# Neighbourhood-attention heads get their own block of 128 rows in DRAM: one load a tile, stores in halves of 64 rows

## The chip, the cores and the metric

The kernel runs on one core of one Trainium2 chip. The metric is device time in microseconds (us) of that core. Before the change the median of 3 runs is 2555.72 us (2554.66 to 2556.14).

## The reference: what is computed

One layer of a trunk over 1024 latent tokens (a 16 x 64 grid) and 256 context tokens, width 1024, all in float32: half a SwiGLU step, then two token mixers on one normalised input, then another half SwiGLU step. The mixers are a two-dimensional neighbourhood attention (8 heads of 64; every latent query looks at a window of 8 x 16 of its grid neighbours, with a bias, and at all 256 context keys, in one softmax) and a latent attention (MLA, 8 heads), joined by sigmoid gates. The part that matters here:

```python
qa, ka, va, cq, ckv, kr, gates = jnp.split(h @ w_in, IN_SPLITS, axis=-1)
...
s_loc = jnp.einsum('bjqhd,bjakhd->bhjqak', q_r, k_b) + bias      # 8 rows x 32 columns of keys, masked to 16
s_ctx = jnp.einsum('bjqhd,bkhd->bhjqk', q_r, k_ctx)
p = jax.nn.softmax(jnp.concatenate([s_loc, s_ctx], axis=-1), axis=-1)
o = einsum('bhjqak,bjakhd->bjqhd', p_loc, v_b) + einsum('bhjqk,bkhd->bjqhd', p[..., n_loc:], v_ctx)
```

Matrix products are made in a reduced format (fp32r) of which a float32 number takes two parts, a high and a low one; a product is made of the parts that matter.

## The kernel before

The program is one straight stream. Two orders matter. Most of it is recorded by a planner (steps of TensorE work, with side work of the other engines and loads spread over them) and pinned: engines execute it in the order in which it was written. The neighbourhood attention's vector and scalar work (lines 1934 to 2027) is written through `nc.vector`, `nc.scalar` and so isn't pinned; a scheduler places it. All loads and stores are issued by SyncE (SP), whose queue is pinned; at most 8 of its transfers are outstanding, since a transfer waits for the one issued 8 before it. A store isn't issued at once: it waits in a list for 2 or 3 steps (or until a load asks for the same tensor), so that SP doesn't stand still for a result.

- **Projections (about 700 to 1180 us of the span).** Units of one weight block each make a 128 x 512 result in a PSUM bank. `emit_q` (line 1376) scales it by 1/8, casts it to the high part `hi` on ScalarE (ACT) and takes the low part `lo` on VectorE (DVE); both are stored in `qas[i]` (pair of heads `i`, 4 pairs, two chunks `ci` of 512 tokens). `emit_k` (line 1394) does the same for keys, in `kas[i]`; `side_k` (line 1605) for the 256 context tokens. In DRAM a tensor of before is [high/low, 128 rows, tokens], and the 128 rows are the 2 x 64 rows of two heads.
- **Neighbourhood attention (about 1284 to 1475 us).** `NaHead.loads` (line 1719) fills a head's tiles. `q` holds the 64 rows of the high queries twice (rows 0 to 63 and 64 to 127), `ql` the low ones twice, `k` the high keys above the low keys, `kvc` the same for context keys and, in its other half, values. So a product over 128 rows adds high x high and high x low at once. A head of 64 rows lies in half of a block of before: every tile takes two loads of 64 rows, 8 a head; the two halves of `k` (256 KB each) come last. Tiles `w` have 6 buffers, two heads of 3.
- **One item** is a quarter of a head (16 columns of the grid), 32 in all. `scores` (line 1971) has TensorE (PE) make for each half s the context scores (`cs`, both halves in one PSUM bank) and the local scores (`loc`, a bank for each half). DVE adds the bias and takes the maximum (line 1995, "I" here, 384 wide), copies the context scores with their maximum (line 1966, "T", 256 wide), joins the maxima (line 2002); ACT makes the exponentials (line 2004). `values` turns the weights by TensorE, splits them (ACT line 2026, DVE line 2027, three times an item: local, context, edge) and weighs the values. `head_out` copies on ACT (lines 1934 to 1938), adds on DVE (line 1939), and multiplies and splits on GpSimd. PE works on scores of a later item while the others finish the earlier. The first three items of head 0 are begun earlier, in the MLA query projection, and use a pool `f`; the scores' bank of one item comes free by the I or T that reads it.
- Loads of the head after next are issued by SP along the items; what SP has to wait for is the release of the tile that they fill.

Of the kernel before, what the change touches and what calls it, by code (L numbers as in the profile page):

```python
# [15 lines left out]
P = 128  # L16
# [3 lines left out]
NLAT = 1024  # L20
# [18 lines left out]
def f32(ap):  # L39
    return ap.bitcast(F32)  # L40
# [3 lines left out]
def hybrid_block(ctx: ExitStack, tc: tile.TileContext, a: dict, out: bass.AP):  # L44
# [11 lines left out]
    def nm(s):  # L56
        count[0] += 1
        return f"{s}_{count[0]}"
# [8 lines left out]
    def U(dt=F32, key="u"):  # L67
        return pools[key].tile([P, 1024], dt, tag="u", name=nm("x" + key))
# [4 lines left out]
    def W(dt=F32R, key="w", n=1024):  # L73
        return pools[key].tile([P, n], dt, tag=key, name=nm(key))

    def T2(dt=F32, n=512):
        return pools["t"].tile([P, n], dt, tag="t", name=nm("t"))
# [4 lines left out]
    def DR(shape):  # L82
        n = nm("d")
        return dp.tile(shape, F32, tag=n, name=n)
# [37 lines left out]
    def ld(dst, src):  # L122
        for x in [x for x in waiting if x[1].tensor.name == src.tensor.name]:
            waiting.remove(x)
            put(*x[1:])
        return put(dst, src)
# [4 lines left out]
    def put(dst, src):  # L131
        return pin(nc.sync.dma_start(dst, src))

    def store(dst, src, n=2):

        if clock[0] is None:
            return put(dst, src)
        waiting.append((clock[0] + n, dst, src))
# [7 lines left out]
    def later(f, n=0):  # L146

        deferred.append((clock[0] + n, f)) if clock[0] is not None else f()
# [1097 lines left out]
    o = len(plan.main)  # L1246
# [7 lines left out]
    e = len(plan.main)  # L1254
# [56 lines left out]
    o = len(plan.main)  # L1311
# [12 lines left out]
    o, tail = down1.plan(plan)  # L1324
# [35 lines left out]


    zs = [DR([P, NLAT]) for _ in range(16)]
    qas = [DR([2, P, NLAT]) for _ in range(4)]
    kas = [DR([2, P, NLAT + NCTX]) for _ in range(4)]

    def emit_gate(i, ci, x, bank):
        t = T2() if bank else x

        def gate():
            act.activation(t, x, AF.Sigmoid, bias=bg[:, i:i + 1])  # L1370
            store(zs[i][:, ci * 512:(ci + 1) * 512], t)
        behind(bank, gate)

    def emit_q(i, ci, x, bank):
        c0 = ci * 512
        t, hi, lo = T2() if bank else x, T2(F32R), T2(F32R)
        tv = t.rearrange("p (r j c) -> p j r c", r=8, j=4)
        hv = hi.rearrange("p (j r c) -> p j r c", j=4, r=8)
        lv = lo.rearrange("p (j r c) -> p j r c", j=4, r=8)

        def high():
            act.activation(t, x, AF.Copy, scale=0.125)
            act.copy(hv, tv)
            store(qas[i][0, :, c0:c0 + 512], f32(hi))
            later(low, 1)

        def low():
            vec.tensor_tensor(lv, tv, f32(hv), op=ALU.subtract)
            store(qas[i][1, :, c0:c0 + 512], f32(lo))
        later(high)  # L1390

    def emit_k(i, c0, n, x, bank=True):
        hi, lo = T2(F32R)[:, :n], T2(F32R)[:, :n]

        def high():
            act.copy(hi, x)
            store(kas[i][0, :, c0:c0 + n], f32(hi))

        def low():
            vec.tensor_tensor(lo, x, f32(hi), op=ALU.subtract)  # L1400
            store(kas[i][1, :, c0:c0 + n], f32(lo))
        if bank:
            high()
            low()
        else:
            later(high)
            later(low, 1)
# [28 lines left out]
    def emit_lat(d, ci, x, bank):  # L1436
        t, sq = T2() if bank else x, T2()

        def high():
            if bank:  # L1440
                act.copy(t, x)
            store(cqT[d][:, ci * 512:(ci + 1) * 512], t)
            act.activation(sq, t, AF.Square)
            later(add, 1)

        def add():
            if ci in squares:
                vec.tensor_tensor(squares[ci], squares[ci], sq, op=ALU.add)
            else:
                squares[ci] = sq  # L1450
        later(high)

    for p in range(3):
        punits.append(Unit(h2, [wc_cols(2 * p), wc_cols(2 * p + 1)],
                           lambda i, ci, x, bank, p=p: emit_lat(2 * p + i, ci, x, bank)))
# [21 lines left out]
    o = len(plan.main)  # L1477
# [23 lines left out]
    e = len(plan.main)  # L1501
# [43 lines left out]
    class Set:  # L1545
# [16 lines left out]
        def loads(self):  # L1562

            return [lambda j=j: self.load(j) for j in range(2)]
# [50 lines left out]
    o = len(plan.main)  # L1615
# [97 lines left out]
    def value_tile(i):  # L1713
        return W(key=("l", "p", "p", "z", "z")[i % 5])

    class NaHead:


        def loads(self, h):
            self.h = h  # L1720
            i, b = h // 2, (h % 2) * 64
            self.q, self.ql, self.k = q, ql, k = [W() for _ in range(3)]
            self.kvc = kvc = W(key="x" if h % 3 == 2 else "kc")
            for s in range(2):
                o = 64 * s
                ld(f32(q[o:o + 64, :]), qas[i][0, b:b + 64, :])
                ld(f32(ql[o:o + 64, :]), qas[i][1, b:b + 64, :])
                ld(f32(kvc[o:o + 64, 0:256]), kas[i][s, b:b + 64, NLAT:])
            for s in range(2):
                ld(f32(k[64 * s:64 * s + 64, :]), kas[i][s, b:b + 64, :NLAT])  # L1730
            self.bias = []
            self.table(0)
            yield
            self.table(1)
            self.va = va = value_tile(2 * h)
            for j in range(2):
                self.values(va, j)
            yield
            self.table(2)
            ld(f32(kvc[:, 256:512]), vcs[h])  # L1740
            yield
            self.vb = vb = value_tile(2 * h + 1)
            for j in range(2, 4):
                self.values(vb, j)
            yield
# [109 lines left out]
    o = va_at  # L1855
# [9 lines left out]
    o = len(plan.main)  # L1865
# [4 lines left out]
    o = len(plan.main)  # L1870
# [3 lines left out]
    o = len(plan.main)  # L1874
# [3 lines left out]
    o = len(plan.main)  # L1878
# [303 lines left out]
    for e in range(2):  # L2182
        e = U(F32R)
# [125 lines left out]
    for d in range(KD):  # L2309
        o = len(plan.main)  # L2310
# [52 lines left out]
    o = len(plan.main)  # L2363
# [13 lines left out]
    o = len(plan.main)  # L2377
# [4 lines left out]
    e = len(plan.main)  # L2382
# [9 lines left out]
    o, tail = down2.plan(plan)  # L2392
# [134 lines left out]
```

## Time and profile before

| what | us |
|---|---|
| median of 3 runs | 2555.72 |
| span of the profiled execution | 2553.0 |
| TensorE busy in it | 2524.7 (99%) |
| VectorE, ScalarE, GpSimd busy | 1904.4, 1238.4, 239.4 |

The profiled execution's span is 2553.0 us; the median of the runs lies 2.7 us above, for what is outside the span. TensorE ran at its full granted clock in all 40 slices of the page. In names of instructions `t`, `xu`, `w`, `bs` are pools (bs, bm, bv: PSUM banks), `d` is any tensor in DRAM, `in_wc` a weight input; a line is often that of a helper (L161 the matmul, L164 the transpose, L120 a recorded vector or scalar operation, L132 the DMA issue).

### The profile page before, as it was taken

To read this page: it belongs to the slowest core of one execution; us is meant where nothing else is said; L and a number is where in the kernel's file an instruction comes from. 1 tells how busy PE (TensorE), PEld (TensorE's weight loads), DVE (VectorE), ACT (ScalarE), POOL (GpSimd) and SP (SyncE) were. 2 spreads that over 40 slices of the span, in tenths; PEclk is the share of its full clock that TensorE was granted. 3 is DMA by queue.
4 is the path that set the end of the run, shared out by engine and by line. 5 is a ranking of instruction groups with operands and counts; after the bars stand their busy time and mean duration, and the time that the engine had idled before them with its cause. 6 is when DMAs were issued, how large, how long until landed. Compare 5 with 4: busy or idle time off the path is not lost.

```text
span 2553.0 us, 38188 instructions
## 1 busy us (share of the span) xinstructions
PE 2524.7 (99%) x13007; PEld 2146.5 (84%) x13007; DVE 1904.4 (75%) x3652; ACT 1238.4 (49%) x2384; POOL 239.4 (9%) x421
## 2 busy tenths in 40 slices
PE   8999999999999999999999999999999999999998
PEld 6888888888888888889889999988888888888887
DVE  5788887898567687874568988886445888777557
ACT  6622223555346643433438888772355322233633
POOL 1000000000002200001006622220030000000000
PEclk9999999999999999999999999999999999999999
DMA  8477765779576665666899823205135667557655
GB/s 314 161 244 234 243 224 188 274 247 294 182 241 221 245 224 188 226 229 203 277 284 249 233 67 77 77 28 214 67 131 179 212 223 236 183 185 259 240 202 194
DMA packets 275477, 523.33 MB, mean 205 GB/s; under 512 B 33425, under 2 KB 84433, under 8 KB 275281
## 3 DMA queue, kind: packets, MB, share of 16 engines
q1 hardware_dynamic: 275280, 520.88, 61.3%
q8 instruction: 103, 1.69, 0.3%
q14 instruction: 94, 0.76, 0.1%
HBM read 375.47 MB, written 145.29 MB: 204 GB/s over the span
## 4 chain that ended last, share of the span: by engine, by line
PE 87%; ACT 5%; DVE 4%; issue 2%; DMA 1%; SPq 0%; POOL 0%; DVEq 0%; POOLq 0%; ACTq 0%
PE bs L161 33%; PE bm L161 30%; PE bv L161 20%; PE bm L164 2%; ACT xu L2105 2%; PE bs L164 1%; DVE xu L1966 1%; DVE t L2132 1%; ACT t L2131 1%; ACT xu L2004 1%; DVE xv L120 1%; DMA xv<-in_wada 0%; ACT t L2105 0%; ACT t L1938 0%; PE bv L164 0%
## 5 line engine op out<-in xcount | busy, mean ns | idle before, releaser
L120 ACT CAST xu<-t 128x512 fp32r<-128x512 f32 x589 | 345.6, 618 | 669.8 <-DVE t L120 556.1
L161 PE MATMUL bm<-xu,xu 128*128 128x512 f32 (+1 forms) x2442 | 596.5, 389 | 0.5 <-ACT t L120 0.4
L161 PEld LDWEIGHTS bm<-xu,xu 128*128 128x128 f32 x2442 | 450.4, 188 | 91.6 <-ACT t L120 1.7
L120 DVE TENSOR_TENSOR xu<-t,xu 128x512 fp32r<-128x512 f32 x589 | 382.8, 686 | 78.3 <-ACT xu L120 78.0
L161 PE MATMUL bs<-xu,xu 128*128 128x512 f32 (+2 forms) x1581 | 388.4, 385 | 0.0
L161 PE MATMUL bs<-xv,xu 128*128 128x512 f32 x1512 | 363.6, 390 | 0.2 <-DVE t L120 0.2
L161 PEld LDWEIGHTS bs<-xu,xu 128*128 128x128 f32 x1581 | 291.9, 188 | 57.8
L161 PE MATMUL bv<-xv,xu 128*128 128x512 f32 x1342 | 336.1, 390 | 0.0
L161 PEld LDWEIGHTS bs<-xv,xu 128*128 128x128 f32 x1512 | 283.6, 188 | 59.5 <-issue 1.0
L161 PEld LDWEIGHTS bv<-xv,xu 128*128 128x128 f32 x1342 | 251.7, 188 | 51.9
L120 DVE TENSOR_TENSOR xu<-xu,xu 128x512 fp32r<-128x512 f32 x282 | 189.5, 687 | 59.9 <-ACT xu L120 58.9
L120 DVE TENSOR_TENSOR t<-t,t 128x512 f32<-128x512 f32 (+4 forms) x350 | 221.0, 634 | 13.9 <-ACT t L120 8.7
L161 PE MATMUL bv<-xu,xu 128*128 128x512 f32 x722 | 191.5, 390 | 0.0
L120 ACT CAST xu<-xu 128x512 fp32r<-128x512 f32 x282 | 169.2, 619 | 15.2 <-DMA xu<-in_f1w 8.9
L120 POOL TENSOR_SCALAR st<-st 128x1 f32<-128x1 f32 x56 | 23.8, 425 | 1581.9 <-ACT t L120 1234.4
L161 PEld LDWEIGHTS bv<-xu,xu 128*128 128x128 f32 x722 | 135.6, 188 | 28.0
L161 PE MATMUL bm<-t,xu 128*128 128x256 f32 (+1 forms) x920 | 156.9, 333 | 0.0
L161 PEld LDWEIGHTS bm<-t,xu 128*128 128x128 f32 x920 | 137.7, 189 | 18.3
L161 PE MATMUL bs<-w,w 96*128 96x512 f32 (+1 forms) x384 | 145.0, 406 | 3.9 <-DVE st L1995 2.1
L2132 DVE TENSOR_TENSOR t<-bm,t 128x512 fp32r<-128x512 f32 x160 | 109.6, 687 | 28.5 <-ACT t L2131 28.1
L164 PE MATMUL bm<-ident,xu 128*128 128x128 f32 x826 | 126.5, 272 | 0.0
L1966 DVE TENSOR_SCALAR_CACHE_REDUCE xu<-bs 128x512 f32<-128x512 f32 (+1 forms) x186 | 110.2, 599 | 2.3 <-PE bs L161 2.1
(256 smaller groups left out, 3376.3 us busy)
## 6 DMA issues: line engine op xcount, KB each, us to landing
d<-t SPq DMA_DIRECT2D x432, 256.0 KB, 2.9
t<-d SPq DMA_DIRECT2D x348, 256.0 KB, 4.9
xu<-in_f1w SPq DMA_DIRECT2D x104, 512.0 KB, 4.4
xu<-in_f2w SPq DMA_DIRECT2D x58, 512.0 KB, 4.6
t<-in_wada SPq DMA_DIRECT2D x112, 256.0 KB, 4.9
t<-in_f1w SPq DMA_DIRECT2D x77, 256.0 KB, 4.8
t<-in_f2w SPq DMA_DIRECT2D x77, 256.0 KB, 5.2
xu<-in_winT SPq DMA_DIRECT2D x36, 512.0 KB, 5.4
```

What stands on the lines that cost most here:

```text
L120: return lambda *x, **y: pin(f(*x, **y))
L161: return pin(nc.tensor.matmul(o, s, m, start=start, stop=stop, skip_group_check=open_group[0]))
L164: return pin(nc.tensor.transpose(o, x, i))
L1966: nc.vector.tensor_scalar(dst, src, 1.0, FMIN, op0=ALU.mult, op1=ALU.max, accum_out=m)
L2004: soft.append(lambda s=s: nc.scalar.activation(pr[s][:, :640], pr[s][:, :640], AF.Exp, bias=n_[:, s:s + 1], accum_out=l[:, s:s + 1]))
L2105: nc.scalar.activation(x, x, AF.Exp, bias=n_[:, s:s + 1], accum_out=l[:, i:i + 1])
L2131: nc.scalar.copy(t[0], pb)
L2132: nc.vector.tensor_tensor(t[1], pb, f32(t[0]), op=ALU.subtract)
```

## The change

`qas[i]` becomes [head of the pair, high/low, 128 rows, tokens], the 128 rows being the head's 64 rows twice. `kas[i]` becomes [head of the pair, 128 rows, tokens], high rows over low rows. A new helper `store_rows` stores a 128 x n result in halves of 64 rows: a query result in 4 stores of 64 x 512 (each half twice), a key result in 2. `NaHead.loads` then needs one load a tile.

```diff
-    qas = [DR([2, P, NLAT]) for _ in range(4)]
+    qas = [DR([2, 2, P, NLAT]) for _ in range(4)]
     kas = [DR([2, P, NLAT + NCTX]) for _ in range(4)]
+
+    def store_rows(dst, c, x, twice, s=0):
+        for e in range(2):
+            for o in range(2) if twice else (s,):
+                store(dst[e][64 * o:64 * o + 64, c], f32(x[64 * e:64 * e + 64, :]))
...
-            store(qas[i][0, :, c0:c0 + 512], f32(hi))
+            store_rows([qas[i][e, 0] for e in range(2)], slice(c0, c0 + 512), hi, True)
...
-            store(kas[i][0, :, c0:c0 + n], f32(hi))
+            store_rows(kas[i], slice(c0, c0 + n), hi, False, 0)
...
-            i, b = h // 2, (h % 2) * 64
+            i = h // 2
...
-            for s in range(2):
-                o = 64 * s
-                ld(f32(q[o:o + 64, :]), qas[i][0, b:b + 64, :])
-                ld(f32(ql[o:o + 64, :]), qas[i][1, b:b + 64, :])
-                ld(f32(kvc[o:o + 64, 0:256]), kas[i][s, b:b + 64, NLAT:])
-            for s in range(2):
-                ld(f32(k[64 * s:64 * s + 64, :]), kas[i][s, b:b + 64, :NLAT])
+            for s, x in enumerate((q, ql)):
+                ld(f32(x), qas[i][h % 2, s])
+            ld(f32(kvc[:, 0:256]), kas[i][h % 2][:, NLAT:])
+            ld(f32(k), kas[i][h % 2][:, :NLAT])
```

In the whole program 16 query stores become 64, 16 + 8 key stores (latent and context) 32 + 16, and 64 loads of the 8 heads 32. The order of TensorE is the same; SP keeps the order of all else.

SP where the second pair's queries of the last projections are stored, before (`t` are the results, `d_317` and `d_316` blocks of `qas`):

```order
L132 DMA xu_9839<-in_winT 128x1024
L132 DMA d_317<-t_9779 128x512
L132 DMA t_9866<-in_wada 128x512
L132 DMA d_317<-t_9780 128x512
L132 DMA d_317<-t_9806 128x512
L132 DMA t_9892<-in_wada 128x512
L132 DMA d_317<-t_9807 128x512
```

and after, in the same place:

```order
L132 DMA xu_9855<-in_winT 128x1024
L132 DMA d_317<-t_9795 64x512 x4
L132 DMA t_9885<-in_wada 128x512
L132 DMA d_317<-t_9796 64x512 x4
L132 DMA d_317<-t_9822 64x512 x4
L132 DMA t_9917<-in_wada 128x512
L132 DMA d_317<-t_9823 64x512 x4
```

Four issues stand where one stood; what lies between them keeps its place. SP at head 2's loads, before (`z` takes values, `y` the bias tables, `x` is this head's `kvc`; `w` in order q, ql, q, ql, k, k):

```order
L132 DMA z_13122<-d_332 128x512
L132 DMA z_13122<-d_333 128x512
L132 DMA w_13250<-d_317 64x1024
L132 DMA w_13251<-d_317 64x1024
L132 DMA x_13253<-d_321 64x256
L132 DMA w_13250<-d_317 64x1024
L132 DMA w_13251<-d_317 64x1024
L132 DMA x_13253<-d_321 64x256
L132 DMA w_13252<-d_321 64x1024 x2
L132 DMA y_13262<-in_bias 128x768
```

and after:

```order
L132 DMA z_13186<-d_332 128x512
L132 DMA z_13186<-d_333 128x512
L132 DMA w_13314<-d_317 128x1024
L132 DMA w_13315<-d_317 128x1024
L132 DMA x_13317<-d_321 128x256
L132 DMA w_13316<-d_321 128x1024
L132 DMA y_13322<-in_bias 128x768
```

The last key load is the fourth behind the two of `z` in place of the eighth. Since the scheduler places the attention's vector work, its order changes too. DVE at the fourth item (the first after the three early ones), before (`t<-bm` is the split of line 2027):

```order
L2027 TENSOR_TENSOR t_13038<-bm_13039,t_13037 128x512
L1966 TENSOR_SCALAR xu_13048,st_13050<-bs_13047 128x256
L2027 TENSOR_TENSOR t_13064<-bm_13065,t_13063 128x512
L1939 TENSOR_TENSOR t_13086<-t_13086,bv_13032 64x256
L2027 TENSOR_TENSOR xu_12900<-bm_13092,xu_12900 128x2x128
L2027 TENSOR_TENSOR t_13112<-bm_13113,t_13111 128x512
L1995 ISA xu_13048,st_13050<-bs_13053,y_12966 128x384
L1995 ISA st_13050 128x1
L1995 ISA xu_13049,st_13050<-bs_13073,y_12966 128x384
L1995 ISA st_13050 128x1
L1966 TENSOR_SCALAR xu_13049,st_13050<-bs_13047 128x256
```

and after (lines stand 2 further on):

```order
L2029 TENSOR_TENSOR t_13102<-bm_13103,t_13101 128x512
L1997 ISA xu_13112,st_13114<-bs_13117,y_13030 128x384
L1997 ISA st_13114 128x1
L1997 ISA xu_13113,st_13114<-bs_13137,y_13030 128x384
L1997 ISA st_13114 128x1
L2029 TENSOR_TENSOR t_13128<-bm_13129,t_13127 128x512
L1968 TENSOR_SCALAR xu_13112,st_13114<-bs_13111 128x256
L1968 TENSOR_SCALAR xu_13113,st_13114<-bs_13111 128x256
L1941 TENSOR_TENSOR t_13150<-t_13150,bv_13096 64x256
L2004 TENSOR_REDUCE st_13115<-st_13114 128x2
```

The item's two I, which stood behind the next item's first split, now stand behind its own first split. In the later items DVE's order before is `t I T I t T` in three of four and `t I T t I T` in the fourth (then line 1939, line 2002 and the edge's split); after, items of `t I I T t T` and of `t I t I T T` alternate.

DVE in the first item of a later head, one of the fourth kind, before:

```order
L2027 TENSOR_TENSOR t_13270<-bm_13271,t_13269 128x512
L1995 ISA xu_13289,st_13291<-bs_13295,y_13262 128x384
L1995 ISA st_13291 128x1
L1966 TENSOR_SCALAR xu_13289,st_13291<-bs_13288 128x256
L2027 TENSOR_TENSOR t_13306<-bm_13307,t_13305 128x512
L1995 ISA xu_13290,st_13291<-bs_13316,y_13262 128x384
L1995 ISA st_13291 128x1
L1966 TENSOR_SCALAR xu_13290,st_13291<-bs_13288 128x256
```

and after:

```order
L2029 TENSOR_TENSOR t_13330<-bm_13331,t_13329 128x512
L1997 ISA xu_13349,st_13351<-bs_13355,y_13322 128x384
L1997 ISA st_13351 128x1
L1997 ISA xu_13350,st_13351<-bs_13376,y_13322 128x384
L1997 ISA st_13351 128x1
L1968 TENSOR_SCALAR xu_13349,st_13351<-bs_13348 128x256
L2029 TENSOR_TENSOR t_13366<-bm_13367,t_13365 128x512
L1968 TENSOR_SCALAR xu_13350,st_13351<-bs_13348 128x256
```

The second I moves ahead of the first T and of the second split; the last T stays last.

## Rows read from the trace of the kernel before

**Rows 1.** The page's busy times.
```profile
PE 2524.7 (99%) x13007; PEld 2146.5 (84%) x13007; DVE 1904.4 (75%) x3652; ACT 1238.4 (49%) x2384; POOL 239.4 (9%) x421
```

**Rows 2.** Busy time by stretch; last columns granted clock, DMA share, GB/s.
```profile
core 0: us, PE busy (x) PEld busy (x) DVE busy (x) ACT busy (x) POOL busy (x), PEclk, DMA share, GB/s
1338.00:1475.00 137.00, 130.58 (x1010) 126.49 (x1010) 124.81 (x428) 121.13 (x290) 90.12 (x172) 1.00 0.87 230
1361.72:1457.89 96.17, 94.06 (x744) 92.12 (x743) 90.33 (x311) 89.80 (x217) 70.40 (x132) 1.00 0.95 246
```

**Rows 3.** Timeline of PE at the start of neighbourhood attention: start, length, work, idle before.
```profile
1347.98 0.50 PE L161 MATMUL bs<-kc,w 128*128 128x256 f32 x2 [2.56 <-DVE st L1995]
...
1358.12 0.60 PE L161 MATMUL bs<-w,w 128*128 128x384 f32 x2 [1.75 <-DMA w<-d]
```

**Rows 4.** Timeline of PE, one wait of the steady part.
```profile
1378.43 0.62 PE L161 MATMUL bs<-w,w 128*128 128x384 f32 x2 [0.69 <-DVE st L1995]
```

**Rows 5.** Timeline of DVE ahead of PE's first wait.
```profile
1346.27 0.42 DVE L2027 TENSOR_TENSOR xu<-bm,xu 128x256 fp32r<-128x256 f32 x1
1346.76 0.69 DVE L2027 TENSOR_TENSOR t<-bm,t 128x512 fp32r<-128x512 f32 x1
1347.36 0.55 DVE L1995 CUSTOM_DVE_ANT_0 xu<-bs,y 128x384 f32<-128x384 f32 x1
...
1347.84 0.55 DVE L1995 CUSTOM_DVE_ANT_0 xu<-bs,y 128x384 f32<-128x384 f32 x1
...
1348.31 0.42 DVE L1966 TENSOR_SCALAR_CACHE_REDUCE xu<-bs 128x256 f32<-128x256 f32 x1
```

**Rows 6.** Chain that ended last, at PE's second wait.
```profile
1349.74 8.24 DMA w<-d
```

**Rows 7.** Timeline of SP, the issues of head 2's loads.
```profile
1344.57 0.80 SPq L132 DMA_DIRECT2D z<-d  x2
1345.41 1.09 SPq L132 DMA_DIRECT2D w<-d  x2
...
1349.10 1.23 SPq L132 DMA_DIRECT2D w<-d  x2
```

**Rows 8.** Busy time by stretch, where rows of 128 or of 64 are loaded.
```profile
1300.00:1310.00 10.00, 10.00 (x72) 9.41 (x71) 5.47 (x16) 2.46 (x5) 0.00 (x0) 1.00 1.06 399
1395.00:1400.00 5.00, 5.00 (x42) 5.00 (x41) 4.91 (x16) 4.41 (x11) 3.68 (x7) 1.00 1.04 200
```

**Rows 9.** Timeline of SP, two runs of stores.
```profile
1229.79 10.13 SPq L132 DMA_DIRECT2D d<-xu  x16
...
1274.71 7.35 SPq L132 DMA_DIRECT2D d<-t  x10
```

**Rows 10.** Busy time by stretch, in the projections of queries and of keys.
```profile
1042.00:1074.00 32.00, 32.00 (x143) 26.49 (x142) 30.10 (x50) 14.92 (x27) 0.00 (x0) 1.00 0.75 239
1071.00:1099.00 28.00, 28.00 (x129) 23.17 (x129) 22.77 (x39) 10.27 (x18) 0.00 (x0) 1.00 0.67 203
```

**Rows 11.** Timeline of SP, first and last query store and the loads behind.
```profile
1042.75 0.33 SPq L132 DMA_DIRECT2D d<-t  x1
...
1065.10 0.32 SPq L132 DMA_DIRECT2D d<-t  x1
1065.51 2.56 SPq L132 DMA_DIRECT2D xu<-in_wc  x4
...
1068.82 2.51 SPq L132 DMA_DIRECT2D xu<-in_wc  x4
```

**Rows 12.** DVE and PE behind those loads.
```profile
1074.96 0.68 DVE L120 TENSOR_TENSOR t<-bs,t 128x512 f32<-128x512 f32 x1
...
1079.23 0.68 DVE L120 TENSOR_TENSOR t<-xu,xu 128x512 f32<-128x512 f32 x1
...
1077.40 2.88 PE L161 MATMUL bs<-xv,xu 128*128 128x512 f32 x12
```

**Rows 13.** DMA issues of that stretch: KB each, median us to landing.
```profile
xu<-in_wc SPq DMA_DIRECT2D x8, 128.0 KB, 2.8
```

More of the change, by code (lines that the diff above doesn't have):

```diff
@@ L1388, in low @@
             vec.tensor_tensor(lv, tv, f32(hv), op=ALU.subtract)
-            store(qas[i][1, :, c0:c0 + 512], f32(lo))
+            store_rows([qas[i][e, 1] for e in range(2)], slice(c0, c0 + 512), lo, True)
         later(high)
@@ L1396, in high @@
             act.copy(hi, x)
-            store(kas[i][0, :, c0:c0 + n], f32(hi))
+            store_rows(kas[i], slice(c0, c0 + n), hi, False, 0)
         def low():
             vec.tensor_tensor(lo, x, f32(hi), op=ALU.subtract)
-            store(kas[i][1, :, c0:c0 + n], f32(lo))
+            store_rows(kas[i], slice(c0, c0 + n), lo, False, 1)
         if bank:
```

## The prediction, made before the changed kernel ran

> **What bounds the kernel now.** First the page's busy times [rows 1]: TensorE (PE) is busy for 2524.7 of 2553.0 us, so it idles 28.3 us in the whole program. Nothing that the change does alters PE's work; it can win only idle time of PE, and it loses what it makes PE wait. Then busy time by stretch: from 1338 to 1475 us, the neighbourhood attention, PE idles 137.00 - 130.58 = 6.4 us [rows 2], and the reader is to see that this is the one place where the changed loads are used. Then PE's timeline there. Two waits make up most of it: 2.56 us at 1347.98 for line 1995 on DVE and 1.75 us ahead of 1358.12 for a load of `w` [rows 3]. The rest, from 1361.72 to 1457.89 (24 items, 4.0 us each), is 96.17 - 94.06 = 2.1 us [rows 2], in three waits of about 0.7 us for line 1995, of which one is shown [rows 4]. The DMA engines are at 0.95 there, but no wait of PE in that stretch is for a load. Last the projections, where the stores go: from 1042 to 1074 PE is busy all of 32.00 us and DVE 30.10, with the DMA engines at 0.75 [rows 10]. A late load there stops DVE and soon PE; there is no idle time to take it up.
>
> **The wait for a load (1.75 us).** The chain of waits shows the second half of head 2's `k`, 8.24 us on its way from 1349.74 [rows 6]. It is the eighth of eight loads that follow the two of `z` (1344.57) at about 0.6 us an issue [rows 7]. After the change `k` is the fourth: with 0.33 to 0.40 us for an issue of 128 rows [rows 7, 11] it leaves SP at about 1346.7, 3 us earlier. Between 1344.6 and its end the engines then carry two `z` (0.52 MB), q and ql (1.05 MB), context keys (0.13) and `k` (0.52): 2.2 MB. At the rate at which rows of 128 are loaded, 399 GB/s, that is 5.6 us, at that of halves, 200 GB/s, 11 us [rows 8]. So `k` lands at about 1350.5 to 1352, where PE wanted it at 1358.12 - 1.75 = 1356.37, or 1353.8 if the first wait goes as well. The wait goes, with some 2 us to spare: -1.75 us (bounds -1.75 and 0).
>
> **The wait for line 1995 (2.56 us).** The order on DVE makes it: before the fourth item's two I at 1347.36 and 1347.84 stand two splits of the next work (1346.27, 1346.76), and ahead of them an addition that waits for ACT [rows 5]. PE's scores stand behind the bank that the I frees. In the new order both I stand behind the first split of their own item, ahead of its T, as in every other item. What is late next no row tells; every other item runs with waits of 0.7 us at most, so I take the whole 2.56 us, bounds -2.56 and 0.
>
> **The steady items (2.1 us).** An I takes 0.55 us, a split of 512 columns 0.69 [rows 5]; a T 0.42 [rows 5]. In an item of `t I T t I T` the second I ends 0.55 + 0.42 + 0.69 + 0.55 = 2.2 us after the first split, in `t I T I t T` 1.5. In the new order it is 1.1 (`t I I`) and 1.8 (`t I t I`). The worst place becomes 0.4 us better, and comes in every second item instead of every fourth. The last T, R and the line 1939 stay where they were. One wait of 0.7 us in eight items shrinks to at most 0.3. I take -1.2 us. Bounds: -2.1, all of this idle time, and +3 us, if the 0.27 us by which `t I t I` is later than the usual order counts in each of the 12 items that have it.
>
> Attention in all: 1.75 + 2.56 + 1.2 = 5.5 us won (bounds -6.4 and +3).
>
> **The query stores.** Twelve of the sixteen lie between 1042.75 and 1065.10 [rows 11], and each becomes four pieces of 64 rows (512 KB in place of 256). Whole stores of 256 KB went at 7.35 / 10 = 0.735 us each. How fast stores of 64 rows go no row here shows. The nearest rows bound it: half the time of a whole one, 0.37 us a piece, if a half goes at full rate; 0.63 us, the measured time of a 128 KB store in small pieces of rows (10.13 / 16) [rows 9]; and loads of 64 rows, whose 200 GB/s make 0.65 us of 128 KB [rows 8]. I take 0.60, near the loads, since they share the shape. The extra work for the DMA engines is 12 x (4 x 0.60 - 0.735) = 20.0 us. In the stretch 0.25 x 32 = 8.0 us are free [rows 10]. The rest, 12.0 us, pushes what is queued behind: two groups of 4 loads of `in_wc` (issued 1065.51 and 1068.82, landing 2.8 us after the last issue, thus at 1074.1 [rows 11, 13]). DVE uses the second group's at 1079.23 [rows 12]: 5.1 us to spare. DVE would then stand 6.9 us. Behind it queue the additions that make PE's next operands; the one that shows the margin ends at 1074.96 + 0.68 = 1075.64 for PE's group at 1077.40 [rows 12], so 1.8 us. PE loses 6.9 - 1.8 = 5.1 us. At 0.37 a piece the extra work is 12 x 0.745 = 8.9 us, within 8.0 + 5.1, and the loss 0; at 0.65 it is 22.4 us and the loss 7.5. Range 0 to 8, value 5.1. SP itself takes the added 48 - 12 = 36 issues of this stretch at no more than 0.6 us, 22 us, beside its other work; since a transfer also waits for the one 8 before it, this is the same queue and not a second cost.
>
> The trace shows the two rates for loads: 399 GB/s for rows of 128, 200 GB/s for rows of 64 [rows 8]. The Trainium skill, page "SBUF — State Buffer", section "Door 1: The DMA port swizzle (why `[64,N]` ≈ `[32,N]`)", says that a transfer of partitions 0 to 63 reaches only 8 of the 16 ports, and the section "Can I just issue two DMAs to hit both halves?" that two transfers on the two halves share the engines and gain some 6%. For loads the trace agrees; of stores no row here shows it. The rule speaks for the new loads and against the new stores. By it the piece takes at least the 0.60 us that I use; without it 0.37, and the loss would be none.
>
> **The other stores.** The first four query stores lie far ahead, where nothing waits for the queue. The key stores (12 of 16, from 1071 on) move as many bytes as before; at half the rate each costs 2 x 0.60 - 0.735 = 0.47 us more, 5.6 us in all, and the 28 us have 0.33 x 28 = 9.2 us free [rows 10]: nothing, while that cover lasts; gone, it is up to 3 us more behind the first stall. Context keys: 8 small stores where DMA is not full, nothing. Buffers `t` come free only with the last of four pieces; they are later by the same queue, and in the 0 to 8 above.
>
> **Sum.** 2553.0 - 5.5 + 5.1 = 2552.6 us of span, with the 2.7 us outside it (median 2555.72 against a span of 2553.0) 2555.3 us.
>
> **The rivals.**
> - *The stores cost nothing.* If pieces go at full rate, or DVE has more margin than the one row shows, only the attention's gain stays: 2555.7 - 5.5 = 2550.2 us, down to 2549.3 with all 6.4. For it: writing to DRAM is another way through the chip than filling tiles, and the 0.63 us row consists of small pieces. Against: the loads' halving.
> - *The stall is the larger.* At 0.65 us a piece, with the key stores' cover gone and DVE's 1.8 us of margin used up already, PE loses 7.5 + 3 = 10.5 us around 1079 to 1100, and the attention gives back 4.3: 2555.7 + 6.2 = 2561.9 us. It outweighs the gain from an extra DMA time of 8.0 + 5.1 + 1.8 + 5.5 = 20.4 us on. For it: DVE is busy 30.1 of 32 us there. Against: the first pieces start as soon as results exist, and PE would have to lose all that DVE loses.
> - *The order costs.* DVE's and ACT's new order makes PE wait 0.27 us in 12 of the items, and the start's 2.56 us stay in another place. Then the attention stands at -1.75 + 3 = +1.3 us: 2557.0 us without the stores' stall, 2562.1 with it. For it: DVE and ACT are at 0.94 and 0.93 of the stretch [rows 2], so a place in the order counts. Against: the last T and all behind it stay in place.
> - *The loads don't come earlier.* If the 1.75 us stays, since SP reaches these loads only behind the `z` that wait for pool `f`: 2555.3 + 1.75 = 2557.1 us.
>
> **Chances.** Forecast (gain and stall within 5 us of each other) 0.48; stores cost nothing 0.26; larger stall 0.13; order costs 0.07; loads not earlier 0.06. A measurement of this kernel can tell about 0.2%, 5.1 us, from no change: faster is below 2550.6, slower above 2560.8. Faster: most of the second case (0.19) and the lower end of the first (0.08), 0.27. Slower: most of the third (0.09), half of the fourth (0.03), the upper end of the first (0.04), 0.16. The rest, 0.57, is no change. The likeliest case alone spans 2551 to 2560; the range that holds 8 in 10 takes in the second case and half of the third: 2548.8 to 2561.5.
>
> **What would show it.** In the profile after: PE's idle time in the attention down from 6.4 us to about 1, with no wait for `w`, and loads of 128 rows near 400 GB/s. In the projections, `d<-t` pieces of 128 KB at about 0.6 us each, the `in_wc` loads issued some 12 us later, a wait of DVE or ACT for them near 1079 and PE idle about 5 us, where there was none. The forecast is wrong if PE stays full from 1042 to 1180 (the first rival), or if PE's idle time in the attention doesn't fall.

## The result and the profile after

The changed kernel takes 2563.25 us (median of 5 runs, 2562.24 to 2568.0), before it 2555.88 us in the same comparison. The ratio is 1.0034, interval [1.0022, 1.0046]: slower by 5.6 to 11.8 us, where 2555.3 us and a range up to 2561.5 were forecast. The profiled execution's span is 2561.5 us, 8.5 more than before.

The page's busy times of the changed kernel, which answer to [rows 1]:

```profile
PE 2529.0 (99%) x13007; PEld 2146.6 (84%) x13007; DVE 1904.9 (74%) x3652; ACT 1239.5 (48%) x2384; POOL 240.3 (9%) x421
```

TensorE (PE) idles 2561.5 - 2529.0 = 32.5 us, 4.2 more, and it is also busy 4.3 us longer with the same 13007 products. Its order is the same in both, so the start of one and the same product in the two traces tells where the time went:

| the product (start before) | start after | later by | step |
|---|---|---|---|
| 865.18 | 865.93 | 0.75 | +0.7, ahead of any changed store |
| 932.27 | 934.35 | 2.08 | +1.3 |
| 1066.52 | 1070.39 | 3.87 | +1.8 |
| 1080.12 | 1085.00 | 4.88 | +1.0 |
| 1082.84 | 1091.77 | 8.93 | +4.1 |
| 1085.56 | 1096.10 | 10.54 | +1.6 |
| 1266.01 | 1277.81 | 11.80 | +1.3 |
| 1347.98 | 1356.99 | 9.01 | -2.8 |
| 1358.12 | 1367.13 | 9.01 | 0 |
| 1437.53 | 1447.12 | 9.59 | +0.6 |
| 1442.60 | 1451.14 | 8.54 | -1.1 |
| 1460.01 | 1468.86 | 8.85 | +0.3 |

The first step isn't the change's: e6 below, without any changed store, has 0.57 of it, and e9, with changed stores, none. So the stores cost 1.3 + 8.5 + 1.3 = 11 us, and the attention gave back 11.80 - 8.85 = 2.9. The last product of the program starts 9.0 us later; what lies behind it differs by some 0.5 us from trace to trace, here 0.5 less.

**The query stores.** PE's timeline of the changed kernel; before it had no wait in this stretch [rows 10]:

```profile
1070.39 1.84 PE L161 MATMUL bv<-xv,xu 128*128 128x512 f32 x7 [1.50 <-DVE t L120]
...
1085.00 1.83 PE L161 MATMUL bv<-xv,xu 128*128 128x512 f32 x7 [0.76 <-DVE t L120]
...
1091.77 4.54 PE L161 MATMUL bs<-xu,xu 128*128 128x512 f32 x12 [3.81 <-DVE t L120]
```

What these waited for is on DVE's timeline:

```profile
1068.29 0.75 DVE L120 SCALAR_TENSOR_TENSOR t<-t,sc,t 128x512 f32<-128x512 f32 x1 [2.27 <-DMA t<-in_wada]
...
1080.98 0.69 DVE L120 TENSOR_TENSOR t<-xu,t 128x512 f32<-128x512 f32 x1 [0.78 <-DMA d<-t]
...
1084.16 0.69 DVE L120 TENSOR_TENSOR t<-bv,t 128x512 f32<-128x512 f32 x1 [0.61 <-DMA d<-t]
...
1089.67 0.69 DVE L120 TENSOR_TENSOR t<-xu,xu 128x512 f32<-128x512 f32 x1 [4.22 <-DMA xu<-in_wc]
```

A load of `in_wada` made DVE late by 2.27 us, `in_wc` by 4.22, and twice a result tile of `t` that a store had not left yet, 1.4 together. SP's timeline shows those loads behind or among the stores. The `in_wada` that DVE waited for was issued at 1063.40, behind 24 of the pieces; the first `in_wc` group of [rows 11] was issued at 1065.51 and is now at 1082.23:

```profile
1044.96 2.38 SPq L132 DMA_DIRECT2D d<-t  x4
...
1063.40 0.39 SPq L132 DMA_DIRECT2D t<-in_wada  x1
...
1064.84 2.54 SPq L132 DMA_DIRECT2D d<-t  x4
...
1068.32 10.72 SPq L132 DMA_DIRECT2D d<-t  x16
...
1082.23 2.57 SPq L132 DMA_DIRECT2D xu<-in_wc  x4
...
1085.49 2.51 SPq L132 DMA_DIRECT2D xu<-in_wc  x4
```

Sixteen pieces took 10.72 us, 0.67 each. It is SP's own time that sets this pace for most of the stretch: the first four took 2.38 us, 0.60 each, although they started with no other transfer under way (DMA share 0.00 from 1043 to 1044.9), and from 1070.7 to 1079.1 the profile shows no wait of SP at all. The DMA issues from 1071 to 1079 (KB each, median us to landing) show pieces landing 2.4 us after their issue, so that about four of the allowed eight are under way:

```profile
d<-t SPq DMA_DIRECT2D x13, 128.0 KB, 2.4
```

Busy time by stretch, first where only such pieces run, then behind PE's longest wait:

```profile
core 0: us, PE busy (x) PEld busy (x) DVE busy (x) ACT busy (x) POOL busy (x), PEclk, DMA share, GB/s
1074.00:1080.00 6.00, 6.00 (x29) 4.95 (x27) 6.00 (x11) 2.78 (x5) 0.00 (x0) 1.00 0.94 205
1090.00:1095.00 5.00, 3.23 (x10) 2.62 (x11) 4.26 (x8) 2.23 (x5) 0.00 (x0) 0.78 0.86 241
```

In the first row the DMA engines are at 0.94 and move 205 GB/s; 64-row loads went at 200 [rows 8]. At 205 / 0.94 = 218 GB/s a piece occupies the engines for 0.60 us, so they are hardly faster than SP. In the second row the granted clock (the column before the DMA share) is 0.78: after its 3.81 us of waiting PE is granted half of its clock, 1.2 of 2.4 GHz, for 3.4 us. The group of 12 products at 1091.77 takes 4.54 us, where 12 took 2.88 [rows 12]. That is 1.7 us on top of the waits, and part of the longer busy time; the rest of that isn't traced to one place.

**The early stores and the context keys,** both costed at nothing. DVE's and then PE's timeline behind the first four query results' stores (issued from 909 to 926):

```profile
933.00 0.69 DVE L120 TENSOR_TENSOR t<-xu,xu 128x512 f32<-128x512 f32 x1 [2.21 <-DMA xu<-in_winT]
```

```profile
934.35 3.01 PE L161 MATMUL bs<-xu,xu 128*128 128x512 f32 x12 [1.16 <-DVE t L120]
```

And the waits from 1262 to 1285 us (who waited for what: us in all, times, longest), where the context keys are stored:

```profile
ACT t L120 <- DMA d<-t: 6.8, 5, 2.1
...
PE bs L161 <- DVE t L120: 0.7, 1, 0.7
```

ACT waited 6.8 us in five waits for `t` tiles that stores still held; at the same place in the kernel before it was one wait of 3.3 us.

**The attention.** PE's timeline at its start, which answers to [rows 3]:

```profile
1356.99 0.48 PE L161 MATMUL bs<-kc,w 128*128 128x256 f32 x2
...
1364.69 0.47 PE L161 MATMUL bs<-x,w 128*128 128x256 f32 x2
1367.13 0.60 PE L161 MATMUL bs<-w,w 128*128 128x384 f32 x2 [1.97 <-DVE t L2029]
```

The 2.56 us ahead of the first row are gone. The wait for head 2's keys stays, 1.97 us at 1367.13; the row names DVE, but the line's last `w`, the keys, landed at 1367.00, 0.13 us ahead. SP's timeline shows why it was no earlier ([rows 7] before):

```profile
1356.39 0.80 SPq L132 DMA_DIRECT2D z<-d  x2
1357.23 0.90 SPq L132 DMA_DIRECT2D w<-d  x2
...
1358.65 0.43 SPq L132 DMA_DIRECT2D w<-d  x1
```

The keys are the fourth load now, but SP still reaches the first only at 1357.23, behind the `z` for which it has to wait until 1356.39. Before, `z` was issued at 1344.57; with the delay of 11.8 us that is the same place. The keys' load went out 2.26 us after the first `z` (before 5.17 us) and took 8.35 us to land (before 8.24). Busy time by stretch, from the first `z` to that landing:

```profile
1356.39:1367.00 10.61, 8.78 (x72) 8.54 (x70) 10.33 (x37) 10.25 (x26) 8.01 (x16) 1.00 0.88 300
```

The steady part, about 24 items again:

```profile
1371.80:1467.80 96.00, 95.15 (x743) 92.33 (x743) 90.72 (x312) 89.96 (x216) 70.82 (x132) 1.00 0.75 245
```

Here PE idles 0.85 us, before 2.1 [rows 2]. But the time did not follow: from the product at 1361.72 to the one at 1457.89 it was 96.13 us before, and between the same two it is 95.85 now. The three waits of 0.7 us are gone, and smaller ones have come in other places, at 1447.12 for one, where PE waits 0.18 us for line 1997 (line 1995 before). The waits of TensorE's weight loads (PEld) show it too, before and then after (us in all, times, longest):

```profile
PEld bs L161 <- DVE st L1995: 3.1, 5, 0.9
```

```profile
PEld bs L161 <- DVE st L1997: 2.7, 9, 0.4
```

### The profile page after: what moved, and what is told of

Same layout as the page of the kernel before. It is cut to its first block, busy times and chain, and to the rows that moved or that the text cites. A ratio compares the mean times of both kernels' runs of the same rounds, so it can differ in the third digit from the quotient of the medians.

```text
span 2561.5 us, 38246 instructions
## 1 busy us (share of the span) xinstructions
PE 2529.0 (99%) x13007; PEld 2146.6 (84%) x13007; DVE 1904.9 (74%) x3652; ACT 1239.5 (48%) x2384; POOL 240.3 (9%) x421
## 4 chain that ended last, share of the span: by engine, by line
PE 84%; DVE 6%; ACT 6%; issue 3%; DMA 1%; SPq 0%; POOL 0%; DVEq 0%; POOLq 0%; ACTq 0%
PE bs L161 32%; PE bm L161 30%; PE bv L161 19%; ACT xu L2107 2%; PE bm L164 1%; DVE xu L1968 1%; PE bs L164 1%; ACT t L2133 1%; DVE t L2134 1%; DVE t L120 1%; DVE xv L120 1%; DMA xu<-in_winT 1%; ACT t L2107 1%; SPq L132 0%; ACT t L1940 0%
```

## The experiments

In all of them TensorE's order is that of before; where loads are one a tile, VectorE's and ScalarE's order is that of the changed kernel.

**e2: the changed stores alone.** Eight loads of 64 rows a head, from the new layout; the vector order is that of before.

```diff
-            for s, x in enumerate((q, ql)):
-                ld(f32(x), qas[i][h % 2, s])
...
+            for s in range(2):
+                o = slice(64 * s, 64 * s + 64)
+                ld(f32(q[o, :]), qas[i][h % 2, 0, o, :])
+                ld(f32(ql[o, :]), qas[i][h % 2, 1, o, :])
...
```

> The stores of the changed kernel alone: 64 rows each, queries twice, but eight loads of 64 rows a head, and the vector order of before. Theory Q: the loss without the gain, 2563.3 + 3 = 2566 us (2564.5 to 2569), TensorE waiting about 6 us between 1066 and 1092. Rival L: 2555 to 2558 us.

Measured 2567.10 us beside 2555.03 of before, ratio 1.0046 [1.0034, 1.0059]: 12 us for the stores, as theory Q had it. The wait at the attention's start is there with the old order:

```profile
1360.58 0.50 PE L161 MATMUL bs<-kc,w 128*128 128x256 f32 x2 [2.56 <-DVE st L2001]
```

Behind it PE is at half clock for 3.4 us, which it was not behind the same wait of before [rows 2, 3]:

```profile
1362.00:1365.00 3.00, 3.00 (x15) 3.00 (x15) 1.42 (x7) 1.82 (x5) 1.29 (x3) 0.50 1.07 218
```

**e1, e3, e4: blocks of two.** e1 keeps the stores of before and loads a tile from two blocks of 64 rows with one load; e3 and e4 keep the new layout and store 128 rows into two blocks at once, whole or in half columns. The core of e1 and e3:

```diff
+                ld(f32(x), qas[i][s:s + 1, b:b + 64, :].to_broadcast([2, 64, NLAT]))
...
+        for o in range(2) if twice else (s,):
+            store(dst[:, 64 * o:64 * o + 64, c], f32(x))
```

and of e4, in the place of e3's last two lines, with `m` half the columns:

```diff
+        for e in range(2):
+            for o in range(2) if twice else (s,):
+                store(dst[:, 64 * o:64 * o + 64, c.start + e * m:c.start + e * m + m], f32(x[:, e * m:e * m + m]))
```

> The stores of before, and one load a tile all the same: the load reads two blocks of 64 rows (or one block twice) of the old layout. The vector and scalar order of the changed kernel comes with it. Theory Q (the stores of 64 rows cost all of the loss, by making the queue late; loads and order give the 3 us seen in the attention): 2555.9 - 3 = 2552.9 us, 2551 to 2554.5, no wait for in_wc and no wait of TensorE between 1042 and 1100. Rival L (loads or the new order on VectorE cost something too): 2556 us or more, with waits in the attention that before does not have.

> The changed kernel with whole stores: 128 rows at a time into two blocks of 64, so two stores of 256 KB a query result and one a key result; bytes as in the changed kernel. Theory Q, rate of 64 rows (pieces are slow since they hold 64 rows): 12 x 0.735 = 8.8 us of extra work, which the 13 us of cover take, so the attention's gain stays: 2553 us (2551.5 to 2555). Rival B (the doubled bytes are what costs): half of the loss stays, 2557 to 2559 us.

> The changed kernel with as many stores and bytes as it has (four of 128 KB a query result, two a key result), but each of 128 rows and half the columns in place of 64 rows and all columns. Theory Q, rate of 64 rows: a piece takes about 0.37 to 0.45 us in place of 0.62, 2553 to 2556 us, the in_wc loads issued 8 us or more earlier than in the changed kernel. Rival N (the number of issues sets it, whatever their shape): 0.6 us a piece as before, 2561 to 2565 us.

All three expectations failed: 2755.17 us (ratio 1.0780 [1.0765, 1.0795]), 2750.31 (1.0762 [1.0748, 1.0777]) and 2768.04 (1.0832 [1.0818, 1.0847]). They tell nothing on the theories, since a new cost hides all else. Busy time by stretch in e1, while such loads run:

```profile
1390.00:1395.00 5.00, 2.51 (x21) 2.27 (x19) 4.75 (x17) 4.74 (x12) 3.81 (x7) 1.00 0.13 51
1400.00:1405.00 5.00, 0.00 (x0) 0.00 (x0) 0.00 (x0) 0.00 (x0) 0.00 (x0) 0.50 0.13 51
```

The DMA share is 0.13, two engines of sixteen, at 51 GB/s, and PE, waiting, is at half clock. The Trainium skill, page "DMA: Bandwidth & Descriptors", section "Rules for kernel authors", says that the slowest dimension of an access pattern sets how many engines a transfer gets, so that an outer dimension of 2 confines it to at most two; the trace agrees with 0.13. The runs that follow have 64 or 128 outermost.

**e6: one load a tile, stores of before.** The load takes the 64 rows as the outer dimension and the copies as the inner one, so tiles hold their rows in pairs; the products are sums over rows and do not mind.

```diff
-            for s in range(2):
-                o = 64 * s
-                ld(f32(q[o:o + 64, :]), qas[i][0, b:b + 64, :])
...
+            for s, x in enumerate((q, ql)):
+                ld(f32(x), qas[i][s, b].rearrange("(r o) c -> r o c", o=1).to_broadcast([64, 2, NLAT]))
+            ld(f32(kvc[:, 0:256]), kas[i][:, b, NLAT:].rearrange("s r c -> r s c"))
+            ld(f32(k), kas[i][:, b, :NLAT].rearrange("s r c -> r s c"))
```

> The stores and the layout of before; one load a tile that takes a head's 64 rows as the outer dimension and the two copies (high and low, or the same rows twice) as the inner one, so that a tile's rows come in pairs; query and key tiles alike, so the products are the same sums in another order. The vector order is that of the changed kernel. If what made e1 slow is an outer dimension of two (its loads show a DMA share of 0.13, two engines of sixteen), 64 outer rows use all engines again. Theory Q: 2555.5 - 3 = 2552.5 us (2550.5 to 2554), no wait in the projections. Rival L: 2556 us or more.

Measured 2552.23 us (11 runs) beside 2555.76, ratio 0.9986 [0.9977, 0.9995]: as theory Q had it, 3.5 us faster, and PE waits for nothing between 1000 and 1300. In the attention the first wait is gone and the one for the keys is left, here under its own name:

```profile
1355.55 0.59 PE L161 MATMUL bs<-w,w 128*128 128x384 f32 x2 [1.36 <-DMA w<-d]
```

**e7: queries twice, in whole stores.** Two stores of 256 KB a query result, one a key result, into flat blocks; loads as in e6.

```diff
+    def store_rows(dst, c0, x, n, copies):
+        for o in range(copies):
+            store(dst[o, :, c0:c0 + n], f32(x))
...
```

> Each query result stored twice in whole stores of 128 rows (2 of 256 KB), each key result once, into flat blocks; loads in pairs as in e6. Bytes as in the changed kernel. Theory Q (rate of 64-row pieces): 12 x 0.735 = 8.8 us of extra work in the projections, within the 13 us of cover, so 2553 us (2551 to 2555.5). Rival B (the doubled bytes cost): 2557 to 2560 us.

Measured 2551.33 us, ratio 0.9983 [0.9975, 0.9992]: the doubled bytes cost nothing, and rival B is out. Busy time by stretch: PE is busy for all of the 32.00 us, as in [rows 10], with the DMA engines at 0.92 in place of 0.75:

```profile
1042.00:1074.00 32.00, 32.00 (x142) 26.48 (x142) 30.05 (x49) 15.27 (x27) 0.00 (x0) 1.00 0.92 320
```

**e8: four pieces a query result, of 128 rows and half the columns.** Pieces and bytes as in the changed kernel.

```diff
...
+        for o in range(copies):
+            for e in range(2):
+                a = e * n // 2
+                store(dst[o, :, c0 + a:c0 + a + n // 2], f32(x[:, a:a + n // 2]))
...
```

> As many stores and bytes as in the changed kernel, four of 128 KB a query result and two a key result, but each of 128 rows and half the columns into flat blocks; loads in pairs as in e6. Theory Q: 0.37 to 0.45 us a piece in place of 0.62, 2553 to 2557 us. Rival N (number of issues): 0.6 us a piece, 2560 to 2565 us.

Measured 2553.95 us, ratio 0.9995 [0.9986, 1.0003]. With the same number of issues some 9 of the 11 to 12 us are gone, so rival N is out; the other 2.6 us to e7 go with the number and size of the pieces (in the trace PE waits 0.97 us at 1085.38 behind `in_wc`, and the product at 932.27 of before loses 0.9). Eight and then sixteen of its pieces, and the stretch in which the sixteen run:

```profile
1047.43 3.71 SPq L132 DMA_DIRECT2D d<-t  x8
...
1064.83 8.81 SPq L132 DMA_DIRECT2D d<-t  x16
```

```profile
1066.00:1072.00 6.00, 6.00 (x28) 4.96 (x27) 5.26 (x9) 1.67 (x3) 0.00 (x0) 1.00 1.05 367
```

The sixteen take 0.55 us each in place of 0.67, more than the 0.45 expected, the eight 0.46. The engines move 367 GB/s at 1.05 (one load of `in_wada` among the pieces), that is 350 at full use in place of 218: a piece of 64 rows occupies them 1.6 times as long. It also takes SP longer to issue, 0.60 against 0.46 us. e8 changes both, so it shows that the shape of 64 rows is what costs, but not how the cost divides between SP and the engines; in the changed kernel's trace SP is the one that has no wait from 1070.7 on.

**e5: halves of 64 rows, each once.** Two stores of 128 KB a query result; key stores as in the changed kernel.

```diff
...
-            for o in range(2) if twice else (s,):
+            for o in (s,):
...
+                ld(f32(x), qas[i][h % 2, s, 0:64].rearrange("(r o) c -> r o c", o=1).to_broadcast([64, 2, NLAT]))
```

> Stores in halves of 64 rows as in the changed kernel, but each query half once (2 stores of 128 KB a result); loads in pairs from the changed layout. Theory Q: 12 x (2 x 0.62 - 0.735) = 6 us of extra work in the query stretch, within the cover of 13 us; the queue is less late by 15 us, so most of the loss goes: 2554 us (2552 to 2557). If halves cost by themselves, not by the queue's length: 2559 us or more.

Measured 2554.64 us, ratio 0.9997 [0.9988, 1.0006], as theory Q had it. PE has no wait from 1000 to 1250: 64-row halves cost nothing there as long as the queue's cover takes them. Of the 2.5 us between the profiled runs of e5 and e6, 1.3 lie at 1266, where the same product starts that much later (1267.87 against 1266.58); some 1.1 lie behind the last product and aren't traced. ACT's waits from 1258 to 1270:

```profile
ACT t L120 <- DMA d<-t: 5.0, 3, 2.2
```

e6 has one such wait of 2.2 us. So the context keys' halves have a price that the sum had at nothing.

**e9: query stores as changed, key stores whole.**

```diff
-            store_rows(kas[i], slice(c0, c0 + n), hi, False, 0)
+            store(kas[i][0, :, c0:c0 + n], f32(hi))
...
```

> Query stores as in the changed kernel (four pieces of 64 rows), key stores whole as before; loads in pairs. Which of the stores cost: theory Q says the query stores near 1042 to 1085 make some 10 of the 12 us and the context keys' halves (near 1266, where e5 still lost 1.5 us) the rest: 2563.3 - 1.5 = 2561.8 us (2560 to 2564), with no step near 1266. Rival K (the key stores' halves cost the most): 2553 to 2556 us.

Measured 2565.12 us beside 2555.65, ratio 1.0040 [1.0026, 1.0054], that is 2562.3 to 2569.5: rival K is out, and the step near 1266 is gone (0.2 us in place of 1.3), but the time is above the range given, and in the total these runs don't show what the key stores add. The profiled run was the shortest of the five (2562.68). PE's waits are those of the changed kernel:

```profile
1070.28 1.86 PE L161 MATMUL bv<-xv,xu 128*128 128x512 f32 x7 [1.69 <-DVE t L120]
...
1084.75 1.83 PE L161 MATMUL bv<-xv,xu 128*128 128x512 f32 x7 [0.59 <-DVE t L120]
...
1091.48 1.92 PE L161 MATMUL bs<-xu,xu 128*128 128x512 f32 x6 [3.76 <-DVE t L120]
```

**e10: e6 with the head's loads ahead of `z`.** The first loads of a neighbourhood head go out at the start of the item before; the keys stand ahead of the context keys.

```diff
...
+        if n % 4 == 3 and n // 4 + 2 < NH:
+            na_next(n // 4 + 2)
```

> e6 with a neighbourhood head's first loads (q, ql, k, context keys, first bias table) issued about an item and a half earlier, ahead of the value loads of the z pool that SP has to wait for, and k ahead of the context keys. In e6 TensorE still waits 1.36 us for head 2's k, which lands 0.14 us before the product starts; theory W: k was late since SP stood at z until 1345.2. Then k lands 3 us or more earlier and the wait goes: 2552.2 - 1.4 = 2550.8 us (2549.5 to 2552). Rival: SP is held by something else there, or the earlier loads press on others: 2552 us or more, the wait stays.

Measured 2549.92 us beside 2555.65, ratio 0.9979 [0.9970, 0.9988]: 3.1 to 7.7 us faster than before, the best of all. SP's timeline and the busy time of the attention:

```profile
1338.63 1.82 SPq L132 DMA_DIRECT2D w<-d  x3
1340.54 0.56 SPq L132 DMA_DIRECT2D x<-d  x1
...
1344.56 0.80 SPq L132 DMA_DIRECT2D z<-d  x2
```

```profile
1338.00:1475.00 137.00, 136.01 (x1043) 131.03 (x1043) 128.12 (x440) 125.86 (x302) 93.21 (x176) 1.00 0.70 228
```

The three `w` go out from 1338.63 on, the keys land at 1346.95 where PE wants them at 1353.3, and PE idles 1.0 us in this stretch in place of 6.4 [rows 2]. `z` is issued at 1344.56 as before, so its wait no longer holds the keys. (e10 also puts the keys ahead of the context keys; which of the two was needed isn't shown.)

## Why the prediction was wrong, point by point

- **That stores of 64 rows make the queue late was right; what sets their pace was not, and that the price fitted was luck.** Pieces of 0.60 us were forecast from the rate of the DMA engines, and 0.64 to 0.67 measured (2.54 / 4, 10.72 / 16). The `in_wc` loads were issued 16.7 us later, 14.5 if the 2.2 us that the whole program was late by 1042 are taken off, where 12.0 were forecast; DVE stood for them, as forecast. But the pace was SP's, about 0.60 us an issue, which the prediction called "the same queue and not a second cost". The two prices happen to lie close together, 0.60 us each. e2 against before and e8 against the changed kernel show that it is the 64 rows.
- **The step that failed is the size of the loss, the 5.1 us by which "PE loses 6.9 - 1.8".** It counted one wait of DVE, 6.9 us for `in_wc`. That wait was 4.22 us; but there were 2.27 for `in_wada` before it, a load among the stores, where the sum looked only at what stands behind the last one, and 1.39 for tiles `t`: 7.9 us in all. PE waited 1.50 + 0.76 + 3.81 = 6.1, so the 1.8 us of margin were right. Half clock after the longest wait took 1.7 more, for which the step had no term, and about 0.7 is what PE's work was late beyond the waits. In all 8.5 us by the table, just above the range of 0 to 8, and between the 5.1 of the forecast and the 10.5 of the rival of the larger stall.
- **Two terms of nothing were 1.3 us each.** "The first four query stores lie far ahead, where nothing waits for the queue": a load of `in_winT` was 2.2 us late for DVE. "Context keys: 8 small stores where DMA is not full, nothing": their stores hold tiles `t`, and ACT waits for the tiles, not for the data. e5 has the step at 1266, and e6 and e9, with whole key stores, have none. The step at 932 is in e2, e8, e9 and the changed kernel, and in none of e5, e6 and e7.
- **The latent keys' stores cost nothing,** as forecast: e5 has them in halves and no step between 1071 and 1100.
- **The wait for line 1995 at the start went,** -2.8 us for the 2.56 forecast. It is a wait for DVE, and e2 with the old order keeps 2.56, while e5 to e10, with the new order, lose it.
- **The steady items gave some 0.2 us of the 1.2 forecast.** The idle time went down by 1.25 us, but the start of the products by -0.2 in the table (9.01 to 8.85): what the vanished waits gave, smaller ones took in other places of the new order. So the rival "the order costs" was right in part, though not for the start's 2.56 us.
- **The 1.75 us did not go.** The keys left SP where they were forecast (1358.65 - 11.80 = 1346.85, forecast 1346.7) and came 2.8 us earlier against the rest of the program (1367.00 - 11.80 = 1355.2, before 1357.98), but PE came earlier by the same amount, its first wait being gone. They were forecast at 1350.5 to 1352, from 2.2 MB at close to 399 GB/s; at the other rate of that sum, 11 us, they would land at 1355.6, which the range left out without a reason. The engines moved 300 GB/s, 3.2 MB in place of 2.2: the bias tables `y`, issued behind the keys, landed within 2 us of them (at 1367.85 and 1368.83), so they shared. Why from 1360 to 1362 the engines moved only some 200 GB/s stays open. The rival "the loads don't come earlier" had the outcome; its reason, SP at `z`, was already in the forecast's start at 1344.6, and e10 shows that going ahead of `z` is the cure.
- **Sum by measurement:** 0.7 + 1.3 + 8.5 + 1.3 - 2.9 = 8.9 us at the end of the attention, and 8.5 of span, against -5.5 + 5.1 forecast. The forecast of no change held the gain too high by 2.6 us and the loss too low by 6.

## What to carry to other kernels

A layout that makes loads whole can make stores halves; count both, at the rate of the shape each has and at the time that the issuing engine takes for it, and look at every load queued among the stores, not only at the one behind them. A transfer's outer dimension can do what a second copy in DRAM does: 64 outer rows with two copies inside gave whole loads and whole stores. Where two waits follow one another on the bound engine, removing the first brings it to the second earlier, so the second needs as much more. Less idle time of the bound engine isn't yet less time: compare the starts of the same work.

## What the runs showed of the hardware

- A transfer between 128 rows of a tile and two blocks in DRAM, the two outermost, ran at a DMA share of 0.13 and 51 GB/s (e1), and kernels with such transfers took 195 to 213 us longer; with 64 rows outermost (e6) the same bytes came in time for all products but one.
- Stores of 64 rows ran at 205 GB/s with the engines at 0.94. Stores of 128 rows and 128 KB ran at 367 with the engines at 1.05, one load among them, and whole stores at 320 with the engines at 0.92 (e7, loads among them): the two rates of loads [rows 8] show in stores too, here 1.6 apart.
- SP took about 0.60 us to issue a store of 64 rows x 2 KB behind another, 0.46 for one of 128 rows x 1 KB (e8), and 0.32 to 0.33 for a whole one by itself [rows 11].
- After a wait of 3.8 us TensorE was granted half clock for 3.4 us; after the waits of 1.5 and 0.8 us before it, it was not. In e2 the same followed a wait of 2.56 us, and before a wait of the same length was followed by the full clock.
